# Two-layer decoder trunk on one core: fill dealt by the load of ScalarE and VectorE, and another slot order in the recurrence

## The chip, the cores and the metric

The kernel runs on one core of one Trainium2 chip. The metric is the device time of one execution in microseconds (us). Names in this text: PE is TensorE's matmul side and PEld its weight loads, ACT is ScalarE, DVE is VectorE, POOL is GpSimd, SP is SyncE (it issues the DMAs). fp32 matmuls are written as sums of products of a high part and a low part in a narrower type, so most operands exist twice (whi and wlo, hh and hlo, pth and ptl, y1h and y1l): the high part is a copy by ACT, the low part a subtraction by DVE or POOL.

## The reference, cut to what matters

One sequence of 1024 positions, width 1024, two layers. Layer 0 is attention with two groups of eight heads: A, a sliding window of 128 with a sink and a position bias, and B, forgetting attention over the whole causal prefix. Layer 1 is a gated linear recurrence.

```python
# layer 0, group B, query block n of 128 (group A: the same on a band of 256 keys, plus bias and sink)
s = q[n] @ k[: kend].T * HEAD_DIM ** -0.5
p = softmax(where(spos <= tpos, s + F[t] - F[s], -inf))          # F = cumsum(log_sigmoid(f))
out[n] = p @ v[: kend]
y = concat(a_out, b_out) * silu(gate);  x = x + g0 * (y @ w_out)

# layer 1
xr, gate = split(h @ w_in);  xc = conv4(xr) + conv_b
r, i = sigmoid(xblk @ w_a + b_a), sigmoid(xblk @ w_x + b_x)      # 8 diagonal blocks of 128
a = exp(-LRU_C * r * softplus(-lam))
u = sqrt(1 - a ** 2) * (i * xc)
h_t = a_t * h_(t-1) + u_t                                        # scan over positions
y = h * silu(gate);  x = x + g1 * (y @ w_out)
```

Each layer is preceded by a norm with a scale and shift that depend on the condition c; a last norm follows.

## The kernel before, in words

All operations are issued through small queue objects (line 85), so the profile shows line 85 for nearly all of them, and one goes by tile names.

**Attention** is cut into units. A unit of group A is a pair of heads p and a pair of query blocks j; a unit of group B is one head hx and a pair of query blocks j, four units to a head. Each unit has steps: S (the scores: matmuls sA or sB into PSUM, then DVE adds the mask row and takes the minimum in one operation, then ACT's exp into pA or pB), T (the transposes of the probabilities on PE into ptA or ptB, split by ACT's copy pth and DVE's subtraction ptl), V (the products oA or oB: first with pth, then with ptl) and E (the finish: rbT transposed on PE, then two products into gy, by DVE and by POOL). For group B, S also begins with a DMA of the mask row into pB and a POOL select on it. Two PSUM tiles serve all transposes.

A list of slots sets which step stands where: in each slot at most one S, one T, and the V and E that have come due. Between the steps PE does other matmuls: the fill (tiles ps_fill), which are the projections of later heads and at the end part of the output projection of layer 0; each is one matmul of 512 columns. The function `weave` (line 1060) deals it out: each step has a cost in PE time, and before each slot the fill that is left is spread over the slots that are left so that steps and fill together take the same PE time in every slot, as far as that goes. Within a slot the fill is spread evenly behind the steps. PE keeps the order in which the code is written; the orders of ACT, DVE, POOL and SP in attention are chosen by the scheduler.

**The recurrence** goes over eight blocks of 128 channels, c = 0 to 7, one slot each: `slot(c)` for 0 to 6 and `last_slot(7)`. Here all engines keep the written order. Slot c does on PE the gates of block c (psr, psi), the projection of block c+2 (ps_lx, both halves of the sequence), and the projection of its gate (ps_lg, both halves). On the other engines it does sigmoids r_r and i_r (ACT), tanh (th_r, ACT), the exp a_r (ACT), its square (ACT), th_r on DVE, the root (ACT), a product and the scan hs_r (DVE), and the convolution of block c+2 (ACT copies xc_r, DVE taps). `gate_s` is the sigmoid sg_r on ACT and its product on DVE, `gate_a` the product of sg_r with hs_r on POOL, `gate_b` the copy y1h on ACT and the subtraction y1l on POOL; each goes by halves of the sequence. `split_next` makes two halves of a weight tile (whi_lg or whi_lx on ACT, wlo_lg or wlo_lx on POOL), `split_r` the blocks for the gates (wrh_r on ACT, wrl_r on POOL). ACT needs other function tables for exp and root than for the sigmoid, so each slot has three table loads.

**The output projection** (ps_o) follows at once. Its first AHEAD tiles leave out the last of eight k-steps, which needs block 7 of the recurrence, and are completed later. Its weights wo are split by `split_out`, on POOL or, for tile 1, on DVE.

Of the kernel before, what the change touches and what calls it, by code (L numbers as in the profile page):

```python
# [22 lines left out]
AHEAD = 3  # L23
RUN = 32
P = 128
S = 1024
D = 1024
KT = D // P
# [20 lines left out]
def hybrid_trunk(  # L49
# [713 lines left out]
    def unit_a(p, j, q, kh, kl, out):  # L763
# [65 lines left out]
        def end():  # L829
# [4 lines left out]
            "S": [(0.43, lambda r=r: score(r)) for r in two],  # L834
            "T": [(0.43, lambda r=r: turn(r)) for r in two],
            "V": [(0.43, lambda r=r: product(r)) for r in two],
            "E": [(0.22, end)],
# [10 lines left out]
    def unit_b(p, hd, j, src, out):  # L848
# [61 lines left out]
        def end():  # L910
            finish(out()[0], box["rb"], 4 + p, j, f"B_{p}_{j}")

        return {
            "S": [
                (2 * max(b - a, 128) / 2400, lambda r=r, i=i: score(r, i))
                for r in range(2) for i, (a, b, _) in enumerate(pieces(2 * j + r))
            ],
            "T": [(0.43, lambda m=m: turn(m)) for m in range(j + 1)],
            "V": [(0.43, lambda m=m: product(m)) for m in range(j + 1)],
            "E": [(0.22, end)] if hd else [],  # L920
# [139 lines left out]
    def weave(slots, gen, total, first=0):  # L1060


        cost = [sum(c for c, _ in s) for s in slots]
        left = total - sum(next(gen) for _ in range(first))
        for i, slot in enumerate(slots):
            rest = sorted(cost[i:])
# [10 lines left out]
            for _, f in slot:  # L1077
# [367 lines left out]
    load_row(1)  # L1445
# [18 lines left out]
    def slot(c):  # L1464
# [41 lines left out]
        if n < KT:  # L1506
            gate_b(c, 0)
        mod_late(c)
        lgs[c, 1] = proj1(0, f"lg_{c}", 1, w)

    def last_slot(c):
# [14 lines left out]
        gate_a(c - 1, 1)  # L1526
# [10 lines left out]
        split_out(2)  # L1537
# [4 lines left out]
        split_out(3)  # L1542
# [9 lines left out]
    for t0, tw in ((0, 512), (512, 256), (768, 256)):  # L1552
# [7 lines left out]
        for e in range(KT):  # L1560
# [4 lines left out]
            ps = (ps_s, ps_t)[e % 2](nm) if t0 == 0 and e <= AHEAD else ps_1(nm)  # L1565
# [100 lines left out]
```

## Time and profile before

| | |
|---|---|
| median of 3 runs | 886.59 us (886.31 to 886.68) |
| the profiled execution | 888.44 us |
| span in its profile | 886.7 us |
| mean granted clock of PE | 0.986 |
| PE busy | 860.7 us, 97% |
| ACT busy | 535.7 us, 60% |
| DVE busy | 564.5 us, 64% |
| POOL busy | 378.1 us, 43% |

The profile is one execution. Times in the views count from the start of its span; the 1.7 us between span and execution lie around it. Attention goes from about 160 to 530 us, the recurrence from 602 to 780, the output projection and the last norm follow. Busy time of PE counts what is in its pipe, so a small idle time in a stage is a true stand of PE, and a granted clock of 0.50 means that PE ran at half speed in that window. "Idle before" is the time for which an engine had nothing running before an instruction, with the instruction that ended last among those it waited for.

### The profile page before, as it was taken

What the parts mean: (1) busy time and instruction counts of PE and PEld (TensorE: products, weight loads), DVE (VectorE), ACT (ScalarE), POOL (GpSimd) and SP (SyncE); (2) the same over time, 40 slices, a digit from 0 to 9 for tenths busy, and PEclk for the clock granted to TensorE, in tenths of its full rate; (3) what the DMA queues carried; (4) which work ended last, traced back from release to release, by engine and by line L of the source; (5) the groups of instructions that cost most, each with busy time, mean ns of one, the idle gap of its engine ahead of it and who ended that gap; (6) DMA issues with size and microseconds to landing.
All of it is one profiled execution on the core that took longest, in us unless ns stands there. A gap on an engine that the chain in (4) does not pass through costs nothing.

```text
span 886.7 us, 13483 instructions
## 1 busy us (share of the span) xinstructions
PE 860.7 (97%) x4618; PEld 730.7 (82%) x4618; DVE 564.5 (64%) x1136; ACT 535.7 (60%) x1047; POOL 378.1 (43%) x427
## 2 busy tenths in 40 slices
PE   9999999999989999999999999999899999999995
PEld 8887898888878888888777888878688877878995
DVE  7886657688676565565656668276556666583453
ACT  5765124788676666566656647358666667774432
POOL 4843322343342232331744656532565555475100
PEclk9999999999999999999999999999899999999998
DMA  9944772100013322322373564421212212126042
GB/s 344 404 185 127 216 229 60 49 25 20 30 53 111 107 80 101 123 87 78 110 240 104 184 209 145 145 79 44 78 54 72 77 57 67 56 71 226 7 149 83
DMA packets 54620, 103.83 MB, mean 117 GB/s; under 512 B 6960, under 2 KB 20720, under 8 KB 54040
## 3 DMA queue, kind: packets, MB, share of 16 engines
q1 hardware_dynamic: 53400, 101.93, 34.8%
q10 hardware_dynamic: 1152, 1.05, 0.5%
q8 instruction: 36, 0.59, 0.3%
q14 instruction: 32, 0.26, 0.1%
HBM read 94.02 MB, written 8.93 MB: 116 GB/s over the span
## 4 chain that ended last, share of the span: by engine, by line
PE 66%; ACT 11%; DVE 10%; DMA 5%; POOL 4%; issue 3%; SPq 0%; DVEq 0%; POOLq 0%; ACTq 0%
PE ps_fill L85 22%; PE ps_o L85 10%; PE pst L85 5%; PE ps_o0c L85 5%; PE oB L85 4%; PE sB L85 4%; PE ptB L85 3%; DVE xc_r L85 3%; PE ps_v L85 3%; DVE hs_r L85 2%; DMA ada<-in_ada_dram 2%; PE ps_lx L85 2%; POOL sg_r L85 2%; PE sA L85 2%; PE ps_lg L85 2%
## 5 line engine op out<-in xcount | busy, mean ns | idle before, releaser
L85 PE MATMUL ps_o<-y1h,wo 128*128 128x256 f32 (+1 forms) x336 | 76.8, 323 | 2.2 <-DVE wo L85 1.1
L85 DVE TENSOR_TENSOR ptl_B<-ptB,pth_B 128x512 fp32r<-128x512 f32 (+1 forms) x80 | 50.8, 636 | 36.8 <-ACT pth_B L85 36.3
L85 ACT ACTIVATE pth_B<-ptB 128x512 fp32r<-128x512 f32 (+1 forms) x80 | 44.0, 551 | 44.6 <-PE ptB L85 43.7
L85 ACT ACTIVATE pB<-pB,mnB 128x128 f32<-128x128 f32 (+3 forms) x64 | 49.5, 774 | 31.3 <-DVE mnB L85 25.9
L85 PEld LDWEIGHTS ps_o<-y1h,wo 128*128 128x128 f32 x336 | 56.7, 192 | 7.5 <-ACT wo L85 1.5
L85 POOL TENSOR_SCALAR_AFFINE_SELECT pB<-pB 128x128 f32<-128x128 f32 x64 | 18.8, 296 | 96.3 <-DMA pB<-gd 71.6
L85 PE MATMUL pst<-hh,ws 128*128 128x512 f32 x192 | 55.3, 396 | 0.1
L85 PE MATMUL ps_o<-y1l,wo 128*128 128x256 f32 (+1 forms) x168 | 54.2, 323 | 0.0
L85 PE MATMUL ps_lg<-h1h,wlo_lg 128*128 128x512 f32 x128 | 51.3, 401 | 2.3 <-POOL wlo_lg L85 2.3
L85 PE MATMUL ps_lg<-h1h,whi_lg 128*128 128x512 f32 x128 | 51.4, 401 | 1.9 <-ACT whi_lg L85 1.9
L85 DVE SCALAR_TENSOR_TENSOR xc_r<-ps_lx,col,xc_r 128x509 f32<-128x509 f32 (+2 forms) x48 | 35.7, 745 | 24.6 <-ACT xt_r L85 23.5
L85 PE MATMUL ps_lg<-h1l,whi_lg 128*128 128x512 f32 x128 | 50.8, 397 | 0.0
L85 PE MATMUL ps_lx<-h1l,whi_lx 128*128 128x512 f32 x128 | 50.3, 393 | 0.2 <-POOL h1l L85 0.2
L85 PE MATMUL ps_lx<-h1h,whi_lx 128*128 128x512 f32 x128 | 50.3, 393 | 0.0
L85 PE MATMUL ps_lx<-h1h,wlo_lx 128*128 128x512 f32 x128 | 50.1, 391 | 0.0
L85 DVE CUSTOM_DVE_ANT_0 pB<-sB,pB 128x384 f32<-128x384 f32 (+2 forms) x64 | 35.4, 554 | 19.4 <-PE sB L85 9.3
L85 ACT ACT_TABLE_LOAD x35 | 44.9, 1283 | 3.6 <-issue 1.9
L85 PE MATMUL ptB<-ident,pB 128*128 128x128 f32 x288 | 45.1, 273 | 1.2 <-DVE ptl_B L85 0.7
L85 PEld LDWEIGHTS ptB<-ident,pB 128*128 128x128 f32 x288 | 35.8, 140 | 12.2 <-PE rbT_B L85 1.5
L85 POOL TENSOR_TENSOR wlo_lx<-raw_lx,whi_lx 128x512 fp32r<-128x512 f32 x16 | 30.6, 1929 | 32.0 <-ACT whi_lx L85 30.1
L85 PEld LDWEIGHTS pst<-hh,ws 128*128 128x128 f32 x192 | 35.9, 188 | 9.0 <-DVE mod L85 0.6
L85 ACT ACTIVATE sq_o<-x 128x512 f32<-128x512 f32 (+1 forms) x33 | 18.0, 545 | 33.3 <-DVE x L85 33.1
(313 smaller groups left out, 2838.7 us busy)
## 6 DMA issues: line engine op xcount, KB each, us to landing
ada<-in_ada_dram SPq DMA_DIRECT2D x32, 512.0 KB
x<-in_xT_dram SPq DMA_DIRECT2D x20, 256.0 KB
ada<-in_ada_dram SPq DMA_DIRECT2D x4, 1024.0 KB
pB<-gd SPq DMA_DIRECT2D x8, 512.0 KB
raw_o0a<-in_wo_dram SPq DMA_DIRECT2D x16, 256.0 KB
raw_o0c<-in_wo_dram SPq DMA_DIRECT2D x16, 256.0 KB
x1d<-x SPq DMA_DIRECT2D x16, 256.0 KB
raw_lx<-in_wl_dram SPq DMA_DIRECT2D x16, 256.0 KB
```

What stands on the lines that cost most here:

```text
L85: ins = issue(*args, **kw)
```

## The change

Five edits.

1. AHEAD goes from 3 to 4, and the PSUM pool of the tile with number AHEAD changes with it.
2. Every step of a unit now has three numbers: its PE time, its load on ACT and its load on DVE. `weave` deals the fill so that the PE time of a slot is in proportion to the larger of its two loads, as far as there is fill.
3. In `slot(c)`, the splits of weights (`split_r`, `split_next`) and the load of the next gate blocks stand right behind the sigmoids; `gate_a` of the second half and both `gate_b` of the block before stand behind `split_xc`, ahead of the exp. Before, `gate_b` of the first half stood at the end of the slot before.
4. `load_row` (the DMA of a row for the final modulation) is asked for one slot ahead of its use and not two.
5. In `last_slot`, all `split_out` are on POOL and two of them earlier, and the second half of block 6 is finished later.

```diff
-AHEAD = 3
+AHEAD = 4
@@ unit_a
-            "S": [(0.43, lambda r=r: score(r)) for r in two],
-            "T": [(0.43, lambda r=r: turn(r)) for r in two],
-            "V": [(0.43, lambda r=r: product(r)) for r in two],
-            "E": [(0.22, end)],
+            "S": [(0.48, 1.4, 1.1, lambda r=r: score(r)) for r in two],
+            "T": [(0.43, 0.6, 0.7, lambda r=r: turn(r)) for r in two],
+            "V": [(0.48, 0.8 * r, 0.9 * r, lambda r=r: product(r)) for r in two],
+            "E": [(0.22, 0.0, 0.4, end)],
@@ unit_b
+        def load(n, i, a, b):
+            last = i + 1 == len(pieces(n))
+            return (b - a) / 1100, (0.4 + (n + 1) * 0.12) * last, 0.22 + (b - a) / 930
...
-                (2 * max(b - a, 128) / 2400, lambda r=r, i=i: score(r, i))
+                (*load(2 * j + r, i, a, b), lambda r=r, i=i: score(r, i))
...
-            "T": [(0.43, lambda m=m: turn(m)) for m in range(j + 1)],
-            "V": [(0.43, lambda m=m: product(m)) for m in range(j + 1)],
+            "T": [(0.43, 0.6, 0.7, lambda m=m: turn(m)) for m in range(j + 1)],
+            "V": [(0.48, 0.4 * (m == j), 0.4 * (m == j), lambda m=m: product(m)) for m in range(j + 1)],
@@ weave
-        cost = [sum(c for c, _ in s) for s in slots]
+        cost = [sum(x[0] for x in s) for s in slots]
+        load = [max(sum(x[1] for x in s), sum(x[2] for x in s)) for s in slots]
...
-            level, acc = 0.0, 0.0
-            for n, c in enumerate(rest):
-                level = (left + acc + c) / (n + 1)
-                acc += c
-                if n + 1 == len(rest) or level <= rest[n + 1]:
-                    break
-            give = max(level - cost[i], 0.0)
+            lo, hi = 0.0, 100.0
+            for _ in range(50):
+                mid = (lo + hi) / 2
+                more = sum(max(mid * w - c, 0.0) for c, w in zip(cost[i:], load[i:]))
+                lo, hi = (mid, hi) if more < left else (lo, mid)
+            give = min(max(lo * load[i] - cost[i], 0.0), left)
@@ mod_late, start
-        load_row(c + 2)
...
-    load_row(1)
@@ slot
-        if c == 0:
-            split_next()
-        else:
+        if c:
             gate_s(c - 1, 1)
-            gate_a(c - 1, 1)
         r, i_ = sig_ri(c, ps)
+        split_r(c + 1)
+        if n < KT:
+            load_r(n)
+        split_next()
...
         split_xc(c + 1)
-        split_r(c + 1)
-        if n < KT:
-            load_r(n)
         if c:
+            gate_a(c - 1, 1)
+            gate_b(c - 1, 0)
             gate_b(c - 1, 1)
         act.activation(a_, r, AF.Exp, scale=nsp[:, c : c + 1])
-        if c:
-            split_next()
...
         gate_a(c, 0)
-        if n < KT:
-            gate_b(c, 0)
         mod_late(c)
+        load_row(c + 1)
@@ last_slot
         gate_s(c, 0)
-        gate_a(c - 1, 1)
+        split_out(1)
...
-        gate_b(c - 1, 1)
...
-        split_out(1, dve)
+        split_out(2)
...
-        split_out(2)
+        gate_a(c - 1, 1)
+        split_out(3)
...
-        split_out(3)
+        gate_b(c - 1, 1)
@@ output projection
-            ps = (ps_s, ps_t)[e % 2](nm) if t0 == 0 and e <= AHEAD else ps_1(nm)
+            ps = (ps_s, ps_t)[e % 2](nm) if t0 == 0 and e < AHEAD else ps_1(nm)
```

What it moves, at three places. First PE, in the last unit of B head 1 (ptB_1_3_3 and oB_1_3 are its transposes and products): the rows behind the four transposes of ptB_1_3_2, up to the product with their low part, ptl_B_1_3_2. Before:

```order
L85 MATMUL ps_fill_0_3602<-hh_0_108,wlo_bq_2_1_3340 128x512
L85 MATMUL ps_fill_0_3602<-hlo_0_109,whi_bq_2_1_3339 128x512
L85 MATMUL oB_1_3_3694<-pth_B_1_3_1_3676,vb0_988 128x256 x2
L85 MATMUL oB_1_3_3694<-ptl_B_1_3_1_3677,vb0_988 128x256 x2
L85 MATMUL ps_fill_0_3602<-hh_0_108,whi_bq_2_1_3339 128x512
L85 MATMUL ps_fill_0_3602<-hh_0_108,wlo_bq_2_1_3340 128x512
L85 MATMUL ptB_1_3_3_3718<-ident_75,pB_1_6_3518 128x128
L85 MATMUL ptB_1_3_3_3718<-ident_75,pB_1_7_3565 128x128 x2
L85 MATMUL ps_fill_0_3602<-hlo_0_109,whi_bq_2_1_3339 128x512
L85 MATMUL ps_fill_1_3733<-hh_1_513,whi_bq_2_0_3333 128x512
L85 MATMUL oB_1_3_3694<-pth_B_1_3_2_3706,vb0_988 128x256 x2
L85 MATMUL oB_1_3_3694<-ptl_B_1_3_2_3707,vb0_988 128x256 x2
```

Now:

```order
L85 MATMUL ps_fill_0_3602<-hh_0_108,whi_bq_2_1_3295 128x512
L85 MATMUL oB_1_3_3698<-pth_B_1_3_1_3678,vb0_988 128x256 x2
L85 MATMUL oB_1_3_3698<-ptl_B_1_3_1_3679,vb0_988 128x256 x2
L85 MATMUL ptB_1_3_3_3717<-ident_75,pB_1_6_3515 128x128
L85 MATMUL ptB_1_3_3_3717<-ident_75,pB_1_7_3565 128x128 x2
L85 MATMUL oB_1_3_3698<-pth_B_1_3_2_3708,vb0_988 128x256 x2
L85 MATMUL oB_1_3_3698<-ptl_B_1_3_2_3709,vb0_988 128x256 x2
```

Of the six fill matmuls between those transposes and that product one is left; they went to slots with scores.

Second ACT, in the recurrence, from slot 1 to slot 2 (sg_r are halves of slot 1's gate, r_r, i_r, th_r belong to slot 2, wrh_r and whi_lg are weights for the gates of block 3 and the gate projection of block 2). Before, up to the table load that stands ahead of slot 2's exp:

```order
L85 ACTIVATE y1h<-sg_r_0_7166 128x512
L85 ACTIVATE sg_r_1_7216<-ps_lg_1_7175 128x512
L85 ACTIVATE r_r_7220<-psr_0_7200,col 128x512
L85 ACTIVATE r_r_7220<-psr_1_7201,col 128x512
L85 ACTIVATE i_r_7221<-psi_0_7208,col 128x512
L85 ACTIVATE i_r_7221<-psi_1_7209,col 128x512
L85 ACTIVATE th_r_7226<-r_r_7220,sp 128x1024
L85 ACTIVATE xch_r_7231<-xc_r_7084 128x1024
L85 ACTIVATE wrh_r_7038<-wr_r_7036 128x128
L85 ACTIVATE wrh_r_7042<-wr_r_7040 128x128
L85 ACTIVATE y1h<-sg_r_1_7216 128x512
L85 ACT_TABLE_LOAD
```

Now, up to the last row ahead of that table load:

```order
L85 ACTIVATE r_r_7215<-psr_0_7196,col 128x512
L85 ACTIVATE r_r_7215<-psr_1_7197,col 128x512
L85 ACTIVATE i_r_7216<-psi_0_7204,col 128x512
L85 ACTIVATE i_r_7216<-psi_1_7205,col 128x512
L85 ACTIVATE wrh_r_7024<-wr_r_7022 128x128
L85 ACTIVATE wrh_r_7028<-wr_r_7026 128x128
L85 ACTIVATE whi_lg_0_7233<-raw_lg_0_7040 128x512
L85 ACTIVATE whi_lg_1_7239<-raw_lg_1_7131 128x512
L85 ACTIVATE th_r_7245<-r_r_7215,sp 128x1024
L85 ACTIVATE xch_r_7250<-xc_r_7082 128x1024
L85 ACTIVATE y1h<-sg_r_0_7164 128x512
L85 ACTIVATE y1h<-sg_r_1_7212 128x512
```

The first y1h copy went from ahead of the sigmoids to the place of the second, and the whi_lg pair, which stood behind the exp, now stands behind the sigmoids.

Third POOL at the same place (the first row is the product of slot 1's gate with its scan). Before:

```order
L85 TENSOR_TENSOR sg_r_0_7166<-sg_r_0_7166,hs_r_7095 128x512
L85 TENSOR_TENSOR y1l<-sg_r_0_7166,y1h 128x512
L85 TENSOR_TENSOR sg_r_1_7216<-sg_r_1_7216,hs_r_7095 128x512
L85 TENSOR_TENSOR wrl_r_7039<-wr_r_7036,wrh_r_7038 128x128
L85 TENSOR_TENSOR wrl_r_7043<-wr_r_7040,wrh_r_7042 128x128
L85 TENSOR_TENSOR y1l<-sg_r_1_7216,y1h 128x512
L85 TENSOR_TENSOR wlo_lg_0_7251<-raw_lg_0_7057,whi_lg_0_7250 128x512
L85 TENSOR_TENSOR wlo_lg_1_7257<-raw_lg_1_7133,whi_lg_1_7256 128x512
```

Now:

```order
L85 TENSOR_TENSOR sg_r_0_7164<-sg_r_0_7164,hs_r_7093 128x512
L85 TENSOR_TENSOR wrl_r_7025<-wr_r_7022,wrh_r_7024 128x128
L85 TENSOR_TENSOR wrl_r_7029<-wr_r_7026,wrh_r_7028 128x128
L85 TENSOR_TENSOR wlo_lg_0_7234<-raw_lg_0_7040,whi_lg_0_7233 128x512
L85 TENSOR_TENSOR wlo_lg_1_7240<-raw_lg_1_7131,whi_lg_1_7239 128x512
L85 TENSOR_TENSOR sg_r_1_7212<-sg_r_1_7212,hs_r_7093 128x512
L85 TENSOR_TENSOR y1l<-sg_r_0_7164,y1h 128x512
L85 TENSOR_TENSOR y1l<-sg_r_1_7212,y1h 128x512
```

POOL's weight splits went from between the y1l subtractions and behind them to a place between the two gate products, and both y1l stand at the end.

More of the change, by code (lines that the diff above doesn't have):

```diff
@@ L1060, in weave @@
     def weave(slots, gen, total, first=0):
-        cost = [sum(c for c, _ in s) for s in slots]
+        cost = [sum(x[0] for x in s) for s in slots]
+        load = [max(sum(x[1] for x in s), sum(x[2] for x in s)) for s in slots]
         left = total - sum(next(gen) for _ in range(first))
         for i, slot in enumerate(slots):
-            rest = sorted(cost[i:])
-            level, acc = 0.0, 0.0
-            for n, c in enumerate(rest):
-                level = (left + acc + c) / (n + 1)
-                acc += c
-                if n + 1 == len(rest) or level <= rest[n + 1]:
-                    break
-            give = max(level - cost[i], 0.0)
+            lo, hi = 0.0, 100.0
[4 more added lines that the diff above has]
+            give = min(max(lo * load[i] - cost[i], 0.0), left)
             left -= give
             part = give / max(len(slot), 1)
-            for _, f in slot:
+            for *_, f in slot:
                 f()
```

2 lines of the change are left out of this document (1 added, 1 removed).

## The prediction

> **What bounds the kernel now.** I read the page's engine totals first, then the waits of PE, then PE's busy time stage by stage, then the timelines of the engines that PE waited for. The first row says that the kernel is TensorE's: the rest is 3% and the clock.
>
> ```profile
> PE 860.7 (97%) x4618; PEld 730.7 (82%) x4618; DVE 564.5 (64%) x1136; ACT 535.7 (60%) x1047; POOL 378.1 (43%) x427
> ```
>
> So only PE's holes matter. In the waits of PE, attention first (160 to 540 us), then the recurrence and the start of the output projection (600 to 800), the holes are small and have many owners (total, times, longest; of attention's one row stands for eight like it):
>
> ```profile
> PE oB L85 <- DVE ptl_B L85: 1.4, 2, 1.1
> ...
> PE ps_lg L85 <- POOL wlo_lg L85: 2.3, 3, 0.8
> PE ps_lg L85 <- ACT whi_lg L85: 1.9, 1, 1.9
> PE ps_o L85 <- DVE wo L85: 1.1, 1, 1.1
> PE ps_o L85 <- ACT wo L85: 1.1, 1, 1.1
> ```
>
> The same by stage (columns: window, its length, busy time of PE, PEld, DVE, ACT, POOL, granted clock, DMA). Three windows are attention; then come, from one slot's gate matmuls to the next, the recurrence's slots c=1, 2, 4 and 5, and the first 20 us of ps_o.
>
> ```profile
> 240.00:264.00 24.00, 21.75 (x138) 18.59 (x137) 17.73 (x53) 18.29 (x52) 11.71 (x24) 1.00 0.13 39
> 418.00:432.00 14.00, 12.43 (x62) 10.25 (x61) 7.62 (x16) 8.73 (x20) 11.01 (x15) 0.88 0.29 85
> 442.00:477.00 35.00, 32.16 (x186) 26.83 (x186) 19.68 (x52) 22.08 (x47) 18.13 (x25) 1.00 0.60 196
> 621.36:651.81 30.45, 27.97 (x109) 22.17 (x108) 20.37 (x27) 17.50 (x25) 16.91 (x12) 0.89 0.23 69
> 651.81:676.38 24.57, 24.57 (x109) 20.27 (x108) 14.47 (x18) 17.51 (x25) 14.37 (x10) 1.00 0.22 66
> ...
> 700.98:726.76 25.78, 24.93 (x109) 20.19 (x108) 15.69 (x19) 17.51 (x25) 14.91 (x10) 1.00 0.22 67
> 726.76:752.61 25.85, 25.00 (x109) 20.19 (x108) 15.75 (x19) 17.50 (x25) 14.89 (x10) 1.00 0.21 67
> ...
> 780.00:800.00 20.00, 17.82 (x71) 14.06 (x70) 16.82 (x14) 13.45 (x17) 14.41 (x9) 0.91 0.29 93
> ```
>
> A hole has a second price. Below, each window with little PE work is followed by one at half the clock, and one is not:
>
> ```profile
> 422.15:425.56 3.41, 1.84 (x10) 1.16 (x9) 1.71 (x3) 3.37 (x8) 3.41 (x4) 1.00 0.89 249
> 425.56:428.97 3.41, 3.41 (x12) 3.02 (x11) 3.06 (x6) 1.05 (x4) 3.27 (x5) 0.50 0.16 63
> 452.87:456.28 3.41, 2.26 (x16) 1.84 (x15) 2.03 (x6) 1.58 (x5) 1.26 (x3) 1.00 0.66 234
> 783.96:787.37 3.41, 1.45 (x6) 0.64 (x4) 3.28 (x2) 2.56 (x4) 2.29 (x2) 1.00 0.00 0
> 787.37:790.79 3.42, 3.20 (x8) 2.52 (x9) 2.50 (x4) 2.06 (x3) 1.27 (x1) 0.50 0.44 144
> ```
>
> 3.41 - 1.84 = 1.57 us idle halved the next window; 3.41 - 2.26 = 1.15 did not. Half the clock for 3.41 us costs 1.71 us. The Trainium skill (TensorE: Matmul & The Clock Gate, "Why this matters for your kernels") asks only for no PE gaps over about 3 us; the trace disagrees, since no single hole here was longer than 1.9. By that rule the tail's term below would lack its 0.85, and the time would be 875.1.
>
> **The change, part by part.** Recurrence first. PE's own slot is 24.57 us, so the slots shown lost 5.88 (30.45 - 24.57), 1.21 and 1.28: 8.4 us. The first is 1.9 us of waiting for ACT's whi_lg and 0.6 for POOL's wlo_lg, with the two half-clock windows that a mean clock of 0.89 over 30 us means (3.4); the others are POOL's wlo_lg, 0.8 late each, and what is left is spread over their ends. Why ACT and POOL are late (columns: start, duration, instruction, idle before and its releaser; PE's wait first, then ACT, then POOL):
>
> ```profile
> 637.11 0.75 PE L85 MATMUL ps_lg<-h1h,whi_lg 128*128 128x512 f32 x1 [1.89 <-ACT whi_lg L85]
> ...
> 610.58 1.15 ACT L85 ACTIVATE a_r<-r_r,nsp 128x1024 f32<-128x1024 f32 x1
> ...
> 705.26 0.63 ACT L85 ACTIVATE y1h<-sg_r 128x512 fp32r<-128x512 f32 x1 [6.99 <-POOL sg_r L85]
> ...
> 710.94 0.65 ACT L85 ACTIVATE y1h<-sg_r 128x512 fp32r<-128x512 f32 x1
> 711.61 1.28 ACT L85 ACT_TABLE_LOAD   x1
> 712.90 1.16 ACT L85 ACTIVATE a_r<-r_r,nsp 128x1024 f32<-128x1024 f32 x1
> 713.96 1.13 ACT L85 ACTIVATE whi_lg<-raw_lg 128x512 fp32r<-128x512 f32 x2
> ...
> 625.45 2.26 POOL L85 TENSOR_TENSOR sg_r<-sg_r,hs_r 128x512 f32<-128x512 f32 x1 [2.52 <-DVE sg_r L85]
> ...
> 733.10 1.29 POOL L85 TENSOR_TENSOR sg_r<-sg_r,hs_r 128x512 f32<-128x512 f32 x1
> ...
> 736.79 1.72 POOL L85 TENSOR_TENSOR wrl_r<-wr_r,wrh_r 128x128 fp32r<-128x128 f32 x2 [2.41 <-ACT wrh_r L85]
> ...
> 740.50 2.52 POOL L85 TENSOR_TENSOR wlo_lg<-raw_lg,whi_lg 128x512 fp32r<-128x512 f32 x2 [0.71 <-ACT whi_lg L85]
> ```
>
> In the old order ACT stands 6.99 us at the first y1h copy (it waits for POOL's gate product sg_r), with the second sigmoid of the gate, the next slot's four sigmoids, tanh and exp queued behind it; whi_lg is made behind the exp a_r, at 713.96, and POOL's wlo_lg behind that. In the new one whi_lg and the wrh pair come right behind the sigmoids, POOL's wrl and wlo_lg stand between the two gate products, and both y1h copies wait for POOL just ahead of the exp. That wait moves; it does not go, and what is queued behind it (exp, square, root, and with them DVE's scan) is what the ring holds anyway. The new ring, from exp to exp: in slot 0, where no whi_lg pair stands behind the exp, the first gate product ended 625.45 + 2.26 - 610.58 = 17.13 after it. Then POOL's 1.72 + 2.52 + 1.29, ACT's y1h 0.65 and table load 1.28 make 24.6. The gate product takes 2.26 here and 1.29 at 733.10, where no DVE operation ran beside it; so the ring is 23.6 if it always runs so, and 24.6 + 2 x 0.97 = 26.5 if two of the POOL products that follow meet DVE as well. I take 24.9, one such meeting in three slots, as all rows of the old order show each kind at one length.
>
> That is 0.3 a slot above PE's 24.57, against a reserve: with the whi_lg pair now ahead of it (1.06 by the starts 712.90 and 713.96), slot 0's exp starts at 611.65, wlo_lg is there 17.13 + 1.72 + 2.52 later, at 633.0, and PE, which stood 1.89 before 637.11, is ready for it at 635.2. The reserve of 2 us lasts six slots at 0.3. So the losses of the slots go: 8.4 saved, and more cannot be. load_row costs nothing: one DMA issue of SP per slot, as before, now asked for one slot ahead of its DVE product and not two; if it landed after a whole slot of 24 us, that product would hold up DVE behind the scan, where nothing else is late. The bank condition goes with AHEAD and moves one tile to another PSUM pool, which is free by then.
>
> Tail. PE reaches ps_o 8.4 earlier, at 771.6. What it needs first is the split of wo, which on POOL follows the gate product of slot 6:
>
> ```profile
> 764.61 1.15 ACT L85 ACTIVATE a_r<-r_r,nsp 128x1024 f32<-128x1024 f32 x1
> ...
> 767.78 2.21 DVE L85 SCALAR_TENSOR_TENSOR th_r<-a_r,th_r 128x1024 f32<-128x1024 f32 x1 [4.14 <-ACT a_r L85]
> ...
> 775.50 2.27 POOL L85 TENSOR_TENSOR sg_r<-sg_r,hs_r 128x512 f32<-128x512 f32 x1 [6.58 <-DVE sg_r L85]
> 777.72 3.54 POOL L85 TENSOR_TENSOR wlo_wo<-raw_wo,whi_wo 128x512 fp32r<-128x512 f32 x2
> ```
>
> In the old order that product ended 775.50 + 2.27 - 764.61 = 13.2 after slot 6's exp. Now the whi_lg pair (1.06) no longer stands behind the exp, and DVE's th_r, 2.21 while POOL made wlo_lg, no longer meets it and gains the 1.0 by which met and unmet products differ above: 11.1. By the ring slot 6's exp starts at 611.65 + 6 x 24.9 = 761.1, so the product ends at 772.2, and the first of the wlo_wo pair (1.29 alone, 1.77 here) at 773.5 to 774.0. PE, which needs its first part for its second product, stands about 1.9 (bounds 0 and 3.4), and with even chances a half-clock window follows: 1.9 + 0.85 = 2.75. The old tail lost 1.1 + 1.1 + 1.71 = 3.9 by the rows above; with AHEAD 4 the tile that needs y1's last eighth comes four products' worth later and the splits on POOL are done by then, so nothing follows. DVE no longer splits wo for PE (1.1 of those waits); POOL has that work instead, 1.3 a half, behind y1's. If POOL were late with it, the old 1.1 would come back. Gain 1.2 (3.9 - 2.75; bounds -1.2 and 3.9).
>
> Attention. The dealing changes PE's order only; instructions per engine stay. Heavy slots get more fill, light ones less. Gains: the three windows idle 2.25, 1.57 (plus 1.71 of clock) and 2.84. In the first, last A units move apart (29 rows from one finish to the next become 36, 18 become 28): I take 1.2. In the second, six yh copies stand before pth on ACT; now more of PE's work stands behind them; I take a hole of 0.9 that trips no clock window: 2.4. The third has DVE waiting for a POOL mask whose DMA is late; fill does not hasten that: 0.8. Together 4.4 (bounds 0 and 8.4). Cost: light slots. At a head's last unit (the order's rows in the section on the change) PE has one fill left between ptB's transposes and the oB that reads their low part. The chain, in a place of the trace:
>
> ```profile
> 415.17 0.63 PE L85 MATMUL ptB<-ident,pB 128*128 128x128 f32 x4
> 415.56 0.48 PE L85 MATMUL ps_fill<-hh,whi_bk 128*128 128x512 f32 x1
> ...
> 417.26 0.40 PE L85 MATMUL oB<-pth_B,vb 128*128 128x256 f32 x2
> 417.50 0.40 PE L85 MATMUL oB<-ptl_B,vb 128*128 128x256 f32 x2
> ...
> 415.90 0.60 ACT L85 ACTIVATE pth_B<-ptB 128x512 fp32r<-128x512 f32 x1
> ...
> 416.53 0.69 DVE L85 TENSOR_TENSOR ptl_B<-ptB,pth_B 128x512 fp32r<-128x512 f32 x1 [0.61 <-ACT pth_B L85]
> ```
>
> The last of four transposes starts about 415.5 and ptl ends at 417.22: 1.7 us are needed. By the starts of these rows a transpose takes PE 0.1 us and a pair of oB products 0.24; a fill takes about as much as the pair, as it streams as many columns. Between that transpose and the reader PE now has the transpose, one fill, four products, three transposes and two products: 0.1 + 0.24 + 0.48 + 0.3 + 0.24 = 1.35; before, five fills more, 2.55. Missing: about 0.4, in each of eight heads: 3 us. The scores ahead of ptB have shortened too, by an amount between nothing and the same 3 us; I take 0.4, as the old distances there were longer than their chain by half a microsecond. Net +1.0 (bounds -6 and +5.4).
>
> Sum: 8.4 + 1.2 + 1.0 = 10.6. The profiled execution took 888.44 us (span 886.7) and would take 877.8; the median of the runs is 886.59, so 876.0. A measurement of this kernel can tell about 0.2%, 1.8 us, from no change.
>
> **The rivals.** *Light slots* (0.2): their waits (6 us with the scores) exceed what the heavy slots give back (0 to 4.4). For it: no slack is left at eight places; against: fill that moved is not lost. Time: 8.4 + 1.2 - 6 + 0 to 4.4, so 878.6 to 883; I write 881.
> *The ring becomes the bound* (0.17): POOL's splits, now inside the ring, meet DVE. By the upper row sum the slot is 26.5, 1.9 over PE, less 2 us of slack: 7.7 over five slots, so 876.0 + 7.7 = 883.7. For it: 2.26 against 1.29 above; against: DVE is busy 15 of 25 us. The Trainium skill (SBUF — State Buffer, "SBUF: two separate sides") states the rule: VectorE's operation with two SBUF inputs and GpSimd's lock each other out for a whole instruction. The 2.26 against 1.29 agrees.
> *Both* (0.03): 878.6 to 883 plus 7.7 makes 886.3 and up; I count it as no change.
> *Slower* (0.06): short waits join in one window of a head, beyond the 1.15 to 1.57 us of the clock rows, and halve the next. That costs 1.57 + 1.71 = 3.3 a head in place of 0.4: five heads make 14.5, which eats the rest: 876.0 + 14.5 = 890.5; all eight, 899. Against: in the old trace attention had one such window, and it took 1.57 of idle time in one window.
> That the dealing does nothing is excluded by the order; that the new slot order does nothing, too.
>
> **How the numbers follow.** Forecast 0.54, 872 to 880, at 876.0. The best case, no tail loss and no light waits, is 876.0 - 2.7 - 3 = 870.3. The range 870.0 to 884.0 holds the forecast and the two first rivals; outside are both, slower, and the tips: 0.18. Faster by over 0.2%: 0.54 + 0.2 + 0.17 = 0.91; same 0.03; slower 0.06.
>
> **What would show it.** Right: slots 1 to 6 each 24.6 us with PE busy throughout, ACT's second y1h copy the one that waits; no half-clock windows at 637 to 644 and 425; PE's waits at ps_o from POOL wlo_wo, about 2 us; oB waiting for DVE ptl_B eight times or more, 0.3 to 0.4 each. Wrong: slots of 25.5 or more (ring), clock 0.50 rows inside attention, or ptB waiting for ACT pB some ten times.

## The result, and the profile after

| | before | after |
|---|---|---|
| median | 886.63 us of 4 runs (886.31 to 889.88) | 897.08 us of 4 runs (894.71 to 897.53) |
| ratio | | 1.0105 (95%: 1.0089 to 1.0122) |
| span in the profile | 886.7 us | 894.8 us |
| mean granted clock of PE | 0.986 | 0.991 |

The change made the kernel 1.05% slower: 9.3 us by the ratio, 10.4 by the two medians. The forecast was 876.0, 10.6 faster, with a range that ended at 884.0. PE's busy time grew by 1.7 us (860.7 before) and its idle time by 6.4, so most of the 8.1 us between the two spans is in PE's holes:

```profile
PE 862.4 (96%) x4618; PEld 729.2 (81%) x4618; DVE 564.5 (63%) x1134; ACT 536.8 (60%) x1047; POOL 386.0 (43%) x429
```

The waits of PE, first attention, then the rest (total, times, longest):

```profile
PE ptB L85 <- ACT pB L85: 6.4, 8, 1.9
PE rbT_B L85 <- POOL wlo_o0a L85: 2.0, 1, 2.0
PE oB L85 <- DVE ptl_B L85: 1.7, 8, 0.3
...
PE ps_o L85 <- POOL wlo_wo L85: 1.8, 1, 1.8
PE ps_o L85 <- ACT whi_wo L85: 1.6, 1, 1.6
PE psq_n L85 <- DVE sqa L85: 0.9, 1, 0.9
```

The first of these rows is new. In all of the old attention it read:

```profile
PE ptB L85 <- ACT pB L85: 0.3, 1, 0.3
```

By stage (window, length, busy PE, PEld, DVE, ACT, POOL, granted clock, DMA): three windows of attention at the same places of the work as the prediction's three, then the recurrence's slots c=1, 3, 4 and 5 from gate to gate, then the first 20 us of ps_o. The steps in the three windows are not quite the old ones, since the fill moved between them: the first holds 20 products of group A where the old one held 28, the third 40 of group B where it held 44.

```profile
242.00:264.20 22.20, 21.30 (x127) 18.01 (x126) 14.60 (x43) 15.28 (x44) 9.92 (x20) 1.00 0.11 31
427.20:438.90 11.70, 10.60 (x64) 9.00 (x62) 6.69 (x17) 9.66 (x21) 6.79 (x10) 1.00 0.27 102
450.00:486.60 36.60, 32.23 (x182) 26.50 (x181) 18.58 (x45) 21.24 (x45) 18.01 (x23) 1.00 0.59 188
632.82:657.39 24.57, 24.57 (x110) 20.27 (x108) 15.23 (x19) 16.98 (x25) 14.79 (x10) 1.00 0.23 71
681.96:706.54 24.58, 24.58 (x110) 20.27 (x109) 15.27 (x18) 16.54 (x25) 15.87 (x10) 1.00 0.22 70
706.54:732.12 25.58, 25.19 (x109) 20.11 (x108) 16.26 (x18) 17.54 (x26) 15.87 (x10) 1.00 0.21 67
732.12:757.76 25.64, 25.19 (x109) 20.11 (x108) 16.26 (x18) 17.59 (x26) 15.87 (x10) 1.00 0.21 67
787.35:807.35 20.00, 18.24 (x72) 14.71 (x73) 11.84 (x9) 14.37 (x18) 18.83 (x11) 0.91 0.29 92
```

Three instants cut the 8.1 us between the spans into places: the first gate matmul of slot 1 (621.36 before, 632.82 after), the moment when PE is ready for ps_o (780.00 before; 787.35 less its wait of 1.64, so 785.71, after) and the end.

| place | before | after | difference | forecast |
|---|---|---|---|---|
| up to slot 1's gates (attention) | 621.36 | 632.82 | +11.5 | -1.0 |
| from there to PE ready for ps_o | 158.64 | 152.89 | -5.75 | -8.4 |
| the tail, to the end of the span | 106.7 | 109.1 | +2.4 | -1.2 |
| sum | 886.7 | 894.8 | +8.1 | -10.6 |

0.7 of the first line is there already at the first scores of attention (160.5 before, 161.2 after). All three terms missed on the same side, attention by 12.5 of the 18.7 us. The mean granted clock is better than before while the time is worse: the loss is not throttling.

### The profile page after: what moved, and what is told of

Same layout as the page of the kernel before. It is cut to its first block, busy times and chain, and to the rows that moved or that the text cites. A ratio compares the mean times of both kernels' runs of the same rounds, so it can differ in the third digit from the quotient of the medians.

```text
span 894.8 us, 13493 instructions
## 1 busy us (share of the span) xinstructions
PE 862.4 (96%) x4618; PEld 729.2 (81%) x4618; DVE 564.5 (63%) x1134; ACT 536.8 (60%) x1047; POOL 386.0 (43%) x429
## 3 DMA queue, kind: packets, MB, share of 16 engines
q10 hardware_dynamic: 1152, 1.05, 0.5%
## 4 chain that ended last, share of the span: by engine, by line
PE 70%; issue 7%; ACT 6%; POOL 6%; DVE 5%; DMA 4%; SPq 1%; DVEq 0%; POOLq 0%; ACTq 0%
PE ps_fill L85 18%; PE pst L85 10%; PE ps_lx L85 6%; PE ps_lg L85 6%; PE ps_o0c L85 5%; PE ps_o L85 5%; PE ptB L85 3%; PE sB L85 3%; PE oB L85 3%; PE ps_v L85 3%; DMA pB<-gd 2%; PE ptA L85 1%; PE sA L85 1%; POOL wlo_lg L85 1%; ACT pB L85 1%
## 5 line engine op out<-in xcount | busy, mean ns | idle before, releaser
L85 PE MATMUL ptB<-ident,pB 128*128 128x128 f32 x288 | 47.6, 276 | 8.3 <-ACT pB L85 6.4
L85 PEld LDWEIGHTS ptB<-ident,pB 128*128 128x128 f32 x288 | 34.5, 140 | 21.7 <-ACT pB L85 11.5
L85 DVE CUSTOM_DVE_ANT_0 ada<-ada,crow,col 128x1024 f32<-128x1024 f32 x24 | 31.6, 1340 | 8.8 <-DMA ada<-in_ada_dram 8.8
```

The lines of the kernel that those rows point to most:

```text
L85: ins = issue(*args, **kw)
```

## The experiments

The theory after the result was that edit 2, the dealing, costs some 10 us through slots that are now too short, and that the rest of the change gains little because POOL's splits lengthened the ring. The recorded texts count attention by how far PE's starts fall behind the streaming time of its own instructions: 26.7 us after and 16.1 before. The idle time alone grew less, from 8.5 to 16.3 us between the first scores and slot 1's gates. The reason is in the starts: from 160 to 540 us PE pauses 38 times where it paused 18 times, and each pause takes about 0.2 us more than its idle time (7.3 us in all after, 3.3 before), which the profile counts as busy.

### Which edit costs: one part at a time

**deal_only**: the kernel before with edit 2 alone.

```diff
...
-            give = max(level - cost[i], 0.0)
+            give = min(max(lo * load[i] - cost[i], 0.0), left)
```

> The kernel before with the new dealing of the fill alone (edit 2). Theory (short slots in attention lose it): 886.6 + 10.6 = 897.2, from 895 to 899, since PE fell 26.7 us behind its own work between 160 and 540 us in the changed kernel's trace and 16.1 in the one before. Rival (the recurrence or the output projection loses it): 885 to 888.

Measured 896.50, ratio 1.0112 (1.0098 to 1.0125). The dealing alone makes the whole loss, and its attention shows the same two waits:

```profile
PE ptB L85 <- ACT pB L85: 5.1, 7, 1.9
...
PE oB L85 <- DVE ptl_B L85: 1.5, 7, 0.2
```

**slot_only**: edits 3 and 4 alone, the old dealing and the old tail.

```diff
+        split_r(c + 1)
+        if n < KT:
+            load_r(n)
+        split_next()
...
+            gate_a(c - 1, 1)
+            gate_b(c - 1, 0)
             gate_b(c - 1, 1)
```

> The kernel before with the new slot order of the recurrence alone (edits 3 and 4; AHEAD 3 and the old last slot stay). Theory: the recurrence gives 6 to 8 us and the old tail, which PE then reaches earlier than ACT and POOL can serve it, takes 1 to 4 back: 882, from 879 to 885. Rival (the new ring is itself the bound, so nothing is saved): 886 or more.

Measured 884.94, ratio 0.9980 (0.9970 to 0.9989): inside the expected range, at its upper end. PE waits for whi_wo, wlo_wo and wo at ps_o, 4.4 us in all, where the kernel before lost 2.2 to two waits for wo.

**slot_tail**: edits 1, 3, 4 and 5, only the dealing is the old one.

```diff
-            give = min(max(lo * load[i] - cost[i], 0.0), left)
+            give = max(level - cost[i], 0.0)
```

> The changed kernel with the old dealing of the fill: edits 1, 3, 4 and 5 alone. Theory: 897.1 less the 10.6 of the dealing, 886.5, from 884 to 888, since the new start of the output projection (5.5 us lost there against 3.9) and a wait for the square sum give most of the recurrence's gain back. Rival (tail edits do their work as forecast): 877 to 880.

Measured 884.21, ratio 0.9966 (0.9954 to 0.9979). Recurrence and tail together give 3.0 us in place of the forecast 9.6. The interval overlaps that of slot_only, so a gain of the tail's edits is not shown.

### Why the recurrence gave so little: the ring

The starts of the exp in slots 4 to 6 of the kernel after, and POOL's operations in slot 4:

```profile
725.72 1.15 ACT L85 ACTIVATE a_r<-r_r,nsp 128x1024 f32<-128x1024 f32 x1
751.38 1.16 ACT L85 ACTIVATE a_r<-r_r,nsp 128x1024 f32<-128x1024 f32 x1
777.06 1.15 ACT L85 ACTIVATE a_r<-r_r,nsp 128x1024 f32<-128x1024 f32 x1
...
740.60 2.27 POOL L85 TENSOR_TENSOR sg_r<-sg_r,hs_r 128x512 f32<-128x512 f32 x1 [2.52 <-DVE sg_r L85]
742.83 2.85 POOL L85 TENSOR_TENSOR wrl_r<-wr_r,wrh_r 128x128 fp32r<-128x128 f32 x2
745.64 2.52 POOL L85 TENSOR_TENSOR wlo_lg<-raw_lg,whi_lg 128x512 fp32r<-128x512 f32 x2
748.12 1.29 POOL L85 TENSOR_TENSOR sg_r<-sg_r,hs_r 128x512 f32<-128x512 f32 x1
```

The ring is 25.66 to 25.68 us in every slot. The sum of the prediction holds with one term changed: 740.60 + 2.27 - 725.72 = 17.15 (forecast 17.13), then wrl 2.8 (forecast 1.72), wlo_lg 2.5, gate product 1.29, and y1h and the table load 1.9. The pair wrl takes 2.85 in each of slots 1 to 6, because each of its two halves runs beside a DVE operation on two tiles in SBUF:

```profile
742.25 1.71 DVE L85 TENSOR_TENSOR i_r<-i_r,xc_r 128x1024 f32<-128x1024 f32 x1
743.88 1.48 DVE L85 TENSOR_TENSOR xcl_r<-xc_r,xch_r 128x1024 fp32r<-128x1024 f32 x1
```

A half takes 1.44 to 1.45 us here and 0.46 where it meets none of these. The 1.72 of the forecast was not a length without a meeting either: at 736.79 of the kernel before, one half took 1.30 beside xcl_r and the other 0.46.

**ring_short**: slot_tail with POOL's second gate product back ahead of the splits, so that these leave the ring.

```diff
         if c:
             gate_s(c - 1, 1)
+            gate_a(c - 1, 1)
         r, i_ = sig_ri(c, ps)
...
         if c:
-            gate_a(c - 1, 1)
             gate_b(c - 1, 0)
```

> slot_tail (old dealing, all other edits) with POOL's second gate product back ahead of the weight splits, so that ACT's second y1h copy and the exp no longer wait for wrl and wlo_lg. Theory (the new ring, measured at 25.66 us against PE's 24.57, builds up a lag of 6 us that is paid at ps_o): exp to exp 24.6 us, no wait for wlo_lg, 1 us or less lost at ps_o where it was 6: 884.2 - 1 - 5 = 878, from 876.5 to 880. Rival (ps_o waits because whi_wo stands behind the sigmoids on ACT, whatever the ring): 883 to 885.

Measured 875.06, ratio 0.9856 (0.9841 to 0.9871), below the expected range. POOL makes both gate products in one go, wrl is back at 1.71 (one half still meets i_r), the exp comes every 24.57, which is PE's own slot, and PE waits for nothing from 600 to 790:

```profile
719.08 3.54 POOL L85 TENSOR_TENSOR sg_r<-sg_r,hs_r 128x512 f32<-128x512 f32 x2 [2.52 <-DVE sg_r L85]
723.29 1.71 POOL L85 TENSOR_TENSOR wrl_r<-wr_r,wrh_r 128x128 fp32r<-128x128 f32 x2 [0.68 <-ACT wrh_r L85]
...
704.22 1.16 ACT L85 ACTIVATE a_r<-r_r,nsp 128x1024 f32<-128x1024 f32 x1
728.79 1.16 ACT L85 ACTIVATE a_r<-r_r,nsp 128x1024 f32<-128x1024 f32 x1
...
771.32:791.32 20.00, 20.00 (x90) 16.57 (x89) 11.78 (x9) 12.14 (x16) 15.16 (x11) 1.00 0.51 170
```

The last row is the start of ps_o: it begins at 771.32 (forecast 771.6) and, in contrast to the kernels before and after, has no hole.

### The tail

In the kernel after, PE waits twice at ps_o, with POOL's product of slot 6 and the split of wo beside it:

```profile
787.35 0.50 PE L85 MATMUL ps_o<-y1h,whi_wo 128*128 128x512 f32 x1 [1.64 <-ACT whi_wo L85]
789.61 0.50 PE L85 MATMUL ps_o<-y1h,wlo_wo 128*128 128x512 f32 x1 [1.76 <-POOL wlo_wo L85]
...
786.08 2.24 POOL L85 TENSOR_TENSOR sg_r<-sg_r,hs_r 128x512 f32<-128x512 f32 x1 [8.48 <-DVE sg_r L85]
788.29 3.50 POOL L85 TENSOR_TENSOR wlo_wo<-raw_wo,whi_wo 128x512 fp32r<-128x512 f32 x2
```

**wo_early**: slot_tail with ACT's whi_wo asked for ahead of block 7's sigmoids.

```diff
-        r, i_ = sig_ri(c, ps)
         split_next()
         wout.append(ready.popleft())
+        r, i_ = sig_ri(c, ps)
```

> slot_tail with the split of the first wo tile ahead of block 7's sigmoids, and nothing else. Theory (POOL's late gate product holds wlo_wo): ACT's part of the wait, 1.6 us, goes over to POOL, since wlo_wo still stands behind that product: 883 to 885, the same. Rival (ACT's queue alone): 884.2 - 1.8 and one half-clock window less, 880.5 to 882.5.

Measured 885.15, ratio 0.9982 (0.9970 to 0.9995). ACT's part of the wait went, and POOL's grew by as much and more:

```profile
781.35 0.79 PE L85 MATMUL ps_o<-y1h,wlo_wo 128*128 128x512 f32 x1 [4.68 <-POOL wlo_wo L85]
```

**ring_wo**: ring_short and wo_early together.

```diff
...
+            gate_a(c - 1, 1)
         r, i_ = sig_ri(c, ps)
...
-            gate_a(c - 1, 1)
             gate_b(c - 1, 0)
...
-        r, i_ = sig_ri(c, ps)
         split_next()
         wout.append(ready.popleft())
+        r, i_ = sig_ri(c, ps)
```

> Both of these edits together. Theory (ring): 876.5 to 879.5, no more than 1 us better than ring_short, because whi_wo is then in time anyway. Rival: 880 to 882, as wo_early.

Measured 876.01, ratio 0.9873 (0.9856 to 0.9890): not better than ring_short, which has no wait left there.

**ring_oldtail**: ring_short with the old last_slot and AHEAD of 3 (edits 1 and 5 undone).

```diff
-AHEAD = 4
+AHEAD = 3
...
-        split_out(1)
+        gate_a(c - 1, 1)
```

> ring_short with AHEAD 3 and the old last slot, so that the tail edits (1 and 5) are undone alone. Theory (they take waits for wo and for the last y1 out of ps_o, which come back when PE is early): 875.1 + 3, from 876.5 to 880. Rival (they are worth nothing, as 884.2 against 884.9 with the long ring says): 874.5 to 876.

Measured 874.78, ratio 0.9862 (0.9848 to 0.9877), the same as ring_short. The theory of a gain from the tail's edits falls: what the old tail lost, it lost because the ring ran behind PE, and a short ring mends that without them.

### Why attention lost: two causes, or one

Two places in the kernel after. First, the end of one head's unit: PE goes from the transposes ptB to the products with ptl. Then the scores of another unit, from sB through DVE and ACT to the transposes (start, duration, instruction, idle before and releaser):

```profile
330.98 0.49 PE L85 MATMUL ptB<-ident,pB 128*128 128x128 f32 x3
331.92 0.50 PE L85 MATMUL oB<-ptl_B,vb 128*128 128x256 f32 x2 [0.21 <-DVE ptl_B L85]
336.14 0.40 PE L85 MATMUL sB<-khb,bq 128*128 128x512 f32 x1
336.95 0.69 DVE L85 SCALAR_TENSOR_TENSOR bq<-ps_fill,bq 64x512 fp32r<-64x512 f32 x1 [0.22 <-ACT bq L85]
337.68 0.69 DVE L85 CUSTOM_DVE_ANT_0 pB<-sB,pB 128x512 f32<-128x512 f32 x1
338.41 0.72 ACT L85 ACTIVATE pB<-pB,mnB 128x512 f32<-128x512 f32 x1 [1.08 <-DVE mnB L85]
339.28 0.44 PE L85 MATMUL ptB<-ident,pB 128*128 128x128 f32 x2 [0.88 <-ACT pB L85]
```

From the scores to the transposes it takes 339.28 - 336.14 = 3.1 us here, as DVE first subtracts a projection's part (bq) that the scheduler put ahead of the minimum. PE had work for 2.3.

**vload**: the kernel after with a load of 0.4 on every V step of group B. By the formula of `weave` this lengthens the slots of one transpose step and one product step at a head's end, where oB waited, from 1.06 to 1.5 us, and takes the fill for it mostly from slots with scores.

```diff
-            "V": [(0.48, 0.4 * (m == j), 0.4 * (m == j), lambda m=m: product(m)) for m in range(j + 1)],
+            "V": [(0.48, 0.4, 0.4, lambda m=m: product(m)) for m in range(j + 1)],
```

> The changed kernel with a load of 0.4 put on every V step of group B, not the last of a unit alone, so that slots of transposes and products get fill again and scores less. Theory (short slots): the eight waits of oB for ptl, 3.0 us, go, and ptB's waits for the exp (8.7 us) stay or grow: 897 - 3 = 894, from 892.5 to 895.5. Rival (where the waits stand does not depend on the slots' length): 896 to 898, with oB waiting as often as before.

Measured 894.98, ratio 1.0087 (1.0073 to 1.0101), little less than the kernel after. The wait for ptl went from 1.7 in 8 to 0.6 in 2, that for pB stayed:

```profile
PE ptB L85 <- ACT pB L85: 5.8, 6, 2.4
...
PE oB L85 <- DVE ptl_B L85: 0.6, 2, 0.4
```

So in idle time the wait that the prediction priced at 3 us is the small part (1.7), and the one that it priced at 0.4 the large (6.4). The time of vload is no price of the first, because its attention also has three half-clock windows (at 338.36, 406.63 and 437.35, at most 5.1 us), where the kernel after has none. The first two follow a single wait for pB, of 2.4 and 2.1 us.

**floor**: the kernel after, where no slot gets less than 1.45 us of PE time as long as there is fill. By the formula of `weave` and the code's own costs and loads the slots of group B's middle heads have 0.48 to 2.96 us, where the old formula gave each 1.77.

```diff
-                more = sum(max(mid * w - c, 0.0) for c, w in zip(cost[i:], load[i:]))
+                more = sum(max(max(mid * w, 1.45) - c, 0.0) for c, w in zip(cost[i:], load[i:]))
...
-            give = min(max(lo * load[i] - cost[i], 0.0), left)
+            give = min(max(max(lo * load[i], 1.45) - cost[i], 0.0), left)
```

> The changed kernel with a floor of 1.45 us of PE time under every slot of attention; heavy slots give the fill for it (2.96 becomes 2.67, 0.48 and 1.06 become 1.45). Theory (slots shorter than the chains between their steps): the loss of the dealing goes and the gain of the heavy slots stays, 884 to 888. Rival (the waits come from what the scheduler queues ahead on ACT, DVE and POOL, whatever the slots' length): 893 to 897.

Measured 891.27, ratio 1.0044 (1.0028 to 1.0060): between the two theories. 5.8 us of the loss come back by the medians, the rest does not. PE still waits for pB, 4.6 us in 5, and one such place shows a queue (POOL, DVE and PE in order of time):

```profile
335.14 0.29 POOL L85 TENSOR_SCALAR_AFFINE_SELECT pB<-pB 128x128 f32<-128x128 f32 x1 [1.84 <-PE sB L85]
335.39 0.74 POOL L85 TENSOR_TENSOR gy<-gy,y_B 128x256 f32<-128x256 f32 x1
336.16 0.41 DVE L85 TENSOR_TENSOR y_B<-oB,tmp 64x256 f32<-64x256 f32 x1 [2.81 <-POOL gy L85]
336.51 0.67 DVE L85 CUSTOM_DVE_ANT_0 pB<-sB,pB 128x512 f32<-128x512 f32 x1
338.15 0.33 PE L85 MATMUL ptB<-ident,pB 128*128 128x128 f32 x1 [1.83 <-ACT pB L85]
```

POOL's gy product of a finished unit stands behind POOL's select for a later unit. There is one tile y, so DVE's next y_B cannot be written before that product has read it; DVE stands 2.81 us, the minimum of the scores behind it, then ACT's exp, then PE.

**floor_dve**: floor with that product on DVE.

```diff
-        mul(gp, g, g, y[:, 2 * j : 2 * j + 2].rearrange("p a b -> p (a b)"))
+        mul(dve, g, g, y[:, 2 * j : 2 * j + 2].rearrange("p a b -> p (a b)"))
```

> floor with the second product of every unit's finish (gy by y) on DVE, not on POOL. Theory (what is left of the waits for the exp in floor is a queue: a POOL select waits for its mask row's DMA, the gy product stands behind it, DVE's next y waits for that product, and the minimum of the scores stands behind y): ptB's two waits of 1.8 and 1.6 us go, and one half-clock window with them, 891.3 - 5 = 886, from 884.5 to 888. Rival (the scores' chain itself is too long for the slots): 890 to 893, ptB waiting as before.

Measured 884.24, ratio 0.9968 (0.9955 to 0.9981), just below the expected range. It is what slot_tail, with the old dealing, has (884.21). PE waits for pB 1.9 us in 3, and PE's busy time in attention is again what it was (before, after, floor_dve):

```profile
160.00:529.00 369.00, 361.06 (x2116) 308.65 (x2115) 242.72 (x643) 246.66 (x585) 148.07 (x251) 1.00 0.31 100
```

```profile
160.00:529.00 369.00, 353.54 (x2066) 299.31 (x2065) 236.60 (x630) 240.76 (x575) 143.76 (x247) 1.00 0.29 93
```

```profile
160.00:529.00 369.00, 361.74 (x2119) 307.66 (x2118) 259.37 (x677) 246.93 (x586) 126.28 (x219) 1.00 0.30 100
```

Part of the 7.0 us between floor and floor_dve is clock: floor had two half-clock windows in attention, at most 3.4 us, floor_dve none.

**after_dve**: the kernel after with that product on DVE and no floor.

```diff
-        mul(gp, g, g, y[:, 2 * j : 2 * j + 2].rearrange("p a b -> p (a b)"))
+        mul(dve, g, g, y[:, 2 * j : 2 * j + 2].rearrange("p a b -> p (a b)"))
```

> The changed kernel with the gy product on DVE and no floor. Theory (short slots and the queue are two causes, and in the changed kernel the queue shows at one place, the first head, 1.9 us): 897.1 - 2.5 = 894.6, from 893 to 896, with oB's eight waits for ptl still there. Rival (the queue is the whole cause): 887 to 890.

Measured 893.40, ratio 1.0073 (1.0060 to 1.0086). By the ratios the product's move alone is worth 0.32%, the floor alone 0.61%, both 1.37% (3, 5 and 12 us). That they give more together than apart is the clock, as far as the profiled executions show. Slot 1's gates start at 632.82 in the kernel after, at 628.93 in floor, 631.33 in after_dve and 620.50 in floor_dve. Up to there floor and after_dve each have 6.83 us at half the clock in attention, which cost at most 3.4, and the other two kernels none. With 3.4 taken off, the floor gives 7.3 us, the product's move 4.9 and both 12.3. So the two gains add up, and short slots and the queue are two causes, each of some microseconds. This rests on one execution of each kernel; where the half-clock windows fall can differ from run to run.

### Does anything of the dealing remain

**ring_deal**: the kernel after with the short ring.

```diff
+            gate_a(c - 1, 1)
         r, i_ = sig_ri(c, ps)
...
-            gate_a(c - 1, 1)
             gate_b(c - 1, 0)
```

> The changed kernel with the second gate product back ahead of the weight splits, and nothing else. Theory (the two causes lie in different stages and add up): 897.1 - 9 = 888, from 886.5 to 889.5: the whole change with the recurrence mended is then still no gain, because of the dealing. Rival (they hang together): 890 or more, or under 886.

Measured 885.98, ratio 0.9978 (0.9967 to 0.9989). Against ring_short (875.06) the dealing costs 10.9 us with the short ring; with the long one it cost 12.9 (897.08 less 884.21). The ring's mending in turn gives 11.1 us here and 9.1 with the old dealing, so 885.98 lies just below the expected 886.5 to 889.5, at the edge of the rival's "under 886". The loss of the dealing and that of the ring are separate in the main. They overlap by some 2 us, and no run says why; 0.9 of that may be a wait for DVE's sqa that only kernels with both have.

**ring_short_dve**: ring_short with the gy product on DVE.

```diff
-        mul(gp, g, g, y[:, 2 * j : 2 * j + 2].rearrange("p a b -> p (a b)"))
+        mul(dve, g, g, y[:, 2 * j : 2 * j + 2].rearrange("p a b -> p (a b)"))
```

> ring_short (old dealing) with the gy product on DVE. Theory: one wait of 1.2 us for POOL's gy goes, nothing else in the old dealing hung on it: 874, from 873 to 875.5. Rival (DVE, busier, delays other steps): 876 to 878.

Measured 875.69, ratio 0.9873 (0.9860 to 0.9885): no gain, where 873 to 875.5 had been expected. With equal slots the queue on POOL costs nothing.

**ring_floor_dve**: floor_dve with the short ring.

```diff
+            gate_a(c - 1, 1)
         r, i_ = sig_ri(c, ps)
...
-            gate_a(c - 1, 1)
             gate_b(c - 1, 0)
```

> floor_dve with the short ring, that is dealing by load with a floor and both queues mended. Theory: 886 less the 9.1 us of the ring: 877, from 875 to 879, so not better than equal slots, since no slot's engine load was what PE waited for most. Rival (dealing by load pays once its short slots and queues are mended): 871 to 874.

Measured 875.60, ratio 0.9873 (0.9858 to 0.9887). Dealing by load, once its two losses are mended, is worth what equal slots are worth, and no more. The five versions with the short ring and without the dealing's losses (ring_short, ring_oldtail, ring_wo, ring_short_dve, ring_floor_dve) lie 1.3 to 1.4% under the kernel before, and their intervals overlap.

## Why the prediction was wrong, by its steps

**"The scores ahead of ptB have shortened too, ...; I take 0.4."** This is the step that failed most. The place and the mechanism were named, and its bound of 3 us given, but the value was near the low end, and even the bound was too small. PE waits for pB 6.4 us in 8 waits, before 0.3 in one. Two things were left out: DVE and ACT serve the projections' results in the same queues, so the chain from scores to transposes is 3.1 us in one place shown and not its bare length; and POOL's queue reaches into it through the single y tile. The scheduler's order on DVE and POOL moved with the slots, and the reserve of "half a microsecond" was read off the old order. The step also took short slots for the only cause; floor, after_dve and floor_dve show two.

**The eight waits for ptl, 0.4 each, 3 us.** Right in place and number, and near in size: eight waits with 1.7 us of idle time and, at about 0.2 us a pause, 3.3 in all, where the old attention had two such waits, 1.4 in all. vload took most of them away, but its time does not price them.

**The backlog's gain of 4.4.** The first window idles 0.9 (forecast 2.25 less 1.2) and the second 1.1 without a clock window (forecast 0.9). The third idles 36.60 - 32.23 = 4.4, where 2.84 less 0.8 was forecast. So about half of it came, as far as windows with somewhat different steps can be compared: 1.35 + 2.2 - 1.5 = 2.0. In the third, 2.0 us are one wait, of rbT_B. The view names POOL's wlo_o0a for it, which rbT_B does not read; a ptl_B of DVE, whose reading of ptB rbT_B may have waited for as they share two PSUM tiles, ended 0.07 us earlier. Which of them it was stays open.

**"I take 24.9, one such meeting in three slots."** Mis-sized: 25.66, since both halves of POOL's wrl meet DVE in every slot, 2.85 in place of 1.72. The 1.72 was taken for a length without a meeting, and it already held one. An order that repeats meets the same neighbours each time, so a mean over meetings and none was the wrong kind of number; the bounds 23.6 and 26.5 held it. The reserve lasted three slots instead of six: 24.6 up to c=3, then 25.58 and 25.64. Slots gained 5.75 of 8.4, and what the ring lagged further was paid at ps_o.

**The tail's 2.75.** Of the right kind: slot 6's gate product ended 786.08 + 2.24 - 777.06 = 11.3 after the exp, forecast 11.1. But the exp came later against PE than the ring of 24.9 would have had it. PE waited 1.64 + 1.76, one half-clock window followed (1.7), and a wait of 0.9 for DVE's sqa came. Such a wait (0.2 to 1.1 us) is in every profile with both the new dealing and the long new ring (after, vload, floor, floor_dve, after_dve) and in no other; why is not shown. That makes 6.0 in all, against 3.9 in the old tail. The old tail's two waits for wo did stay away, as "nothing follows" had it. But ring_oldtail shows that they would have gone with a short ring alone.

**The rivals.** *Light slots* was the right story for attention at too low a price (6 us of waits, where attention lost 11.5 in all), *the ring becomes the bound* the right one for the recurrence; both came true, which had been given 0.03 and priced as no change. *Slower* had the sign, but its mechanism is not what happened: the clock in attention of the kernel after is 1.00 throughout. (Variants did have it: vload three half-clock windows there, floor and after_dve two each.) That the dealing can cost 10 us without any clock was not among the cases.

What stays open: how much of the queue's part belongs to the select, to its mask's DMA or to the one y tile. A second y tile and a select on another engine were not tried. That PE pauses more often is counted, but no run prices the 0.2 us a pause apart from the waits.

## What to carry to other kernels

Fill between two steps of a chain is not only work to place but the distance that hides the chain: before dealing it by load, write for each pair of steps the chain's length, with what else stands in those engines' queues, and keep that as a floor. Where an operation is moved into a ring that repeats, price it by the neighbour that it will meet each time, not by a mean; the same move done in another order (gate product ahead of the splits) was worth 9 us. And where a bound of a term is several times its value, and the term occurs at many places, the sum should be made with the bound as well before a chance is put on it.

## What the runs showed of the hardware

**The clock's window.** From attention to the start of ps_o the half-clock stretches last one or two windows of 3.41 us, and the windows lie on a fixed grid: in the kernel before they start at 425.56, 637.19 and 787.37, which is 62 and 44 windows apart. Whether a window is at half the clock seems to depend on PE's idle time, summed, in the window ahead of it. The kernel after, three pairs of neighbouring windows, the first in attention, the second at 455, the third at ps_o:

```profile
274.63:278.04 3.41, 1.80 (x9) 1.24 (x7) 1.67 (x4) 1.84 (x4) 2.22 (x3) 1.00 0.07 27
278.04:281.46 3.42, 3.14 (x18) 2.72 (x19) 2.39 (x7) 2.06 (x5) 0.00 (x0) 1.00 0.24 77
455.54:458.95 3.41, 2.14 (x14) 1.46 (x12) 1.19 (x4) 3.36 (x9) 2.30 (x3) 1.00 0.91 301
458.95:462.36 3.41, 2.73 (x16) 2.41 (x17) 1.29 (x3) 0.80 (x2) 2.12 (x3) 1.00 0.87 290
...
786.62:790.04 3.42, 0.94 (x3) 0.58 (x4) 2.22 (x4) 3.37 (x7) 3.42 (x3) 1.00 0.00 0
790.04:793.45 3.41, 3.41 (x10) 2.64 (x9) 2.83 (x4) 1.96 (x4) 3.41 (x2) 0.50 0.37 120
```

3.41 - 1.80 = 1.61 idle left the clock whole, 2.48 halved it, and 1.57 had halved it in the kernel before. No sharp limit comes out: 1.72 (deal_only, at 454.61) and 1.86 (ring_oldtail, at 452.27) left it whole too, while every window of attention, the recurrence or the start of ps_o with 1.88 or more was followed by half. The single wait of 2.0 us of rbT_B (at about 459) is split over two windows as 1.27 and 0.68 and cost its own length only. So whether a hole costs 1.7 us more depends on where it falls on the grid. The Trainium skill (TensorE: Matmul & The Clock Gate, "Why this matters for your kernels") asks for no gaps over about 3 us. The trace disagrees: in the kernels before and after the clock was halved though no single hole was longer than 2.0 us.

**POOL beside DVE.** One 128x128 subtraction of POOL (half of the pair wrl) takes 0.46 us where DVE is idle, and 1.29 to 1.45 beside a DVE operation on two tiles in SBUF. Beside DVE's convolution taps, which read one of their tiles from PSUM, each half took 0.46 too (605.05 to 605.94 in the kernel after). In slot 4 of the kernel after the pair ends at 745.68, 0.32 us behind DVE's xcl_r. The larger gate product takes 1.29 and 2.27.

**PE's pauses.** In attention a pause costs PE about 0.2 us beyond its idle time, by the distance between the starts on its two sides: 23.0 us for 38 pauses with 15.7 of idle time after, 11.2 for 18 with 7.9 before.
